# An encoder step on one core: the first chunk opened by row blocks, and six of eight output blocks turned by VectorE

## Chip, core and metric

One core of one Trainium2 chip. The metric is the device time of one launch in microseconds (us), median of three runs. TensorE is called PE, VectorE DVE, ScalarE ACT, GpSimd POOL, SyncE SP.

## What is computed

One step of a two-layer streaming encoder on 256 prompt rows and 32 sample rows, model width 1024, all in float32:

```python
def _trunk(x, p, hgrn_state, sb_k, sb_v):
    for l in range(DEPTH):                                  # 2 layers
        x = x + 0.5 * _swiglu(_rms(x, ffn1_norm[l]), ffn1_w_gate[l], ffn1_w_up[l], ffn1_w_down[l])
        h = _rms(x, mix_norm[l])
        y = _mixer_ab(h, ...) if l % 2 == 0 else _mixer_c(h, ...)
        x = x + y
        x = x + 0.5 * _swiglu(_rms(x, ffn2_norm[l]), ffn2_w_gate[l], ffn2_w_up[l], ffn2_w_down[l])
    return x, ...

def _swiglu(x, w_gate, w_up, w_down):                       # 1024 -> 2816 -> 1024
    return (jax.nn.silu(x @ w_gate) * (x @ w_up)) @ w_down
```

Outputs are `x` of the prompt (256 x 1024) and of the sample (32 x 1024), and caches of the mixers, which the change does not touch.

## The kernel before

`x` lives transposed in SBUF: `xT` has 8 blocks `k` of 128 model columns, each 128 partitions x 288 columns (`NT`: 32 sample rows, then 256 prompt rows). Weights are read once, in a fixed stream of chunks of up to 8 blocks of 128 x 256 (1 MB each). `fetch` loads a chunk into one of three `wraw` buffers from SP's queue; `pieces` splits it, two blocks at a time, into a rounded part `wh` (ACT, line 206) and a rest `wl` (DVE, line 207), which go to four `wspl` buffers of half a chunk each. Every block product takes three matmuls per half of the output columns (lines 246 to 248: `wl` with `xh`, `wh` with `xl`, `wh` with `xh`; here called products), so a chunk of 8 blocks is 48 products of 288 columns. `xh` and `xl` are the same split of `x` times the norm's gain (`gained`: ACT line 291, DVE line 292). The norm's factor `rb` is applied when a result leaves PSUM (`evac`).

The order on each engine is the order of the code, with a few things let in between: `tick`, called after each block, advances the split of the next chunk and, at a rate, the steps of a "lane" (`nlane`) that holds the norm (`rnorm`) or the output of a block (`result`). The loads and stores of SP's and ACT's queues use eight semaphores in turn, and an issue waits until the one eight before it has landed.

The opening: `setup` loads the identity, `x_prompt` in halves of 512 columns (rows 0 to 127 from SP's queue, 128 to 255 from ACT's), `x_sample` from POOL's queue and the first weight chunk in halves (`fetch_half`). `first_block` then turns each block `k` by PE transposes (`turn`, line 1143: 128, 128 and 32 rows into one PSUM tile), splits it, and copies it to `xT` (`keep`). `WARM` is the number of filler matmuls on PE, (8, 6): eight at the start, six after four turns (line 1155). The row sums of squares are made by DVE (`first_squares`). Chunk 0 then runs with all its 48 products, and `rb` is made by a matmul (line 328) in the middle of chunk 1.

The closing: the last step of the last layer's second SwiGLU is four column groups `j` of three chunks (8, 8 and 6 blocks), called c0 to c11 here. `last` runs the two halves of the final chunk of a group one after the other, adds each to `xT` (`resid`, line 359), and queues `result(k)`: three PE transposes back to rows (line 1258), an ACT and a DVE copy out of PSUM, one store of the prompt's part on SP's queue (line 1262, pieces of 512 bytes) and one of the sample's on ACT's.

Of the kernel before, what the change touches and what calls it, by code (L numbers as in the profile page):

```python
# [14 lines left out]
P = 128  # L15
D = 1024
# [77 lines left out]
class Net:  # L94
# [89 lines left out]
    def fetch_half(self, j):  # L184

        if j == 0:
            self.raw[0] = self.t(self.wraw, [P, 8, 256], "wraw")
        x = slice(4 * j, 4 * j + 4)
        ap, = self.stream[0]
        self.nc.sync.dma_start(out=self.raw[0][:, x], in_=ap[4 * j * P:4 * j * P + 4 * P].rearrange("(k p) c -> p k c", p=P))  # L190
# [63 lines left out]
    def in_chunk(self):  # L254
        acc = self.pair_ps()
        ch = self.next_chunk()
        self.mm((acc[:, 0], acc[:, 1]), ch, (self.xh, self.xl), self.KORD, True, True)
        self.nlane.drain()
        return acc

    def evac(self, pool, tag, bufs=None):
        acc = self.in_chunk()
        x = self.t(pool, [P, 2, NT], tag, bufs=bufs)
        self.nc.vector.tensor_tensor(out=x, in0=acc[:, :, :NT], in1=self.rb, op=ALU.mult)  # L264
        return x
# [132 lines left out]
    def ffn(self, gnext):  # L398
        nc = self.nc
        with self.tc.tile_pool(name=f"ffn{self.uid}", bufs=2, reuse_waits="tile") as pool:  # L400
            self.hidden(pool, KF)
            for n in range(DFF // 256):
                if n == 3 and not self.lv:
                    self.constants()
                g = self.evac(pool, "g")
                nc.scalar.activation(out=g, in_=g, func=AF.Silu)  # L406
                u = self.evac(pool, "u")
                nc.vector.tensor_tensor(out=u, in0=u, in1=g, op=ALU.mult)  # L408
                self.put(2 * n, u)
# [668 lines left out]
    def setup(self, st):  # L1078
        nc, I, c = self.nc, self.I, self.const
        self.st = st  # L1080
        xs = [self.t(st, [P, 1472 if i == 0 else D], f"xs{i}") for i in range(3)]
        warm = self.t(st, [P, 8], "warm")
        nc.vector.memset(warm, 0.0)
        nc.scalar.activation(out=warm, in_=warm, func=AF.Copy, scale=1.0)
        xp, xq = I["x_prompt"], I["x_sample"]
# [4 lines left out]
        nc.gpsimd.dma_start(out=xs[2][0:TS], in_=xq[0])  # L1090
        nc.sync.dma_start(out=cf, in_=I["cf"][:, :P])
        nc.scalar.dma_start(out=first, in_=I["ffn1_norm"][0].rearrange("(n p) -> n p", p=P))
# [13 lines left out]
        spare = self.pair_ps()  # L1106
        for i in range(self.WARM[0]):
            nc.tensor.matmul(spare[:, 0, :P], lhsT=self.ones, rhs=self.ones, start=True, stop=True)
        self.onr = c.tile([P, P], F32R, name="onr")
# [10 lines left out]
        pr = self.ps("first")  # L1120
        nc.tensor.transpose(pr[:, :8], first, self.ident[:8, :8])
# [5 lines left out]
        with self.tc.manual_schedule(engines={mybir.EngineType.Activation, mybir.EngineType.DVE}):  # L1127
            self.first_block(st, xs, g0, spare)
        self.nlane.rate = 0.5

    WARM = (8, 6)

    def first_block(self, st, xs, g0, spare):

        nc = self.nc
        split = self.ahead = self.pieces(0)
        px = {}

        def turn(k):
            px[k] = self.ps("x")  # L1140
            for w, n in enumerate(ROWS):
                s = WIN[w][0]
                nc.tensor.transpose(px[k][:, s:s + n], xs[w][:n, k * P:k * P + P], self.ident[:n, :n])  # L1143
# [6 lines left out]
        stats = self.first_squares(st, xs)  # L1150
        next(stats)
        for k in range(4):
            turn(k)
# [3 lines left out]
        keep(0, v)  # L1157
        next(split)
        keep(1, a)
        turn(4)  # L1160
        keep(2, v)
        turn(5)
        next(split)
        keep(3, a)
        turn(6)
        next(split)
        turn(7)
        next(stats, None)
        norm = self.rnorm(None)
        next(norm)  # L1170
        self.nlane.todo.append(norm)
        keep(4, a)
        keep(5, a)
        keep(6, a)
        keep(7, a)

    def first_squares(self, st, xs):

        nc = self.nc
        part = self.t(st, [P, 3, 2, 6], "part")  # L1180
        mv = self.t(st, [P, 3, 2], "mv")
        nc.vector.memset(mv, 0.0)
        for i in range(2):
            for w, n in enumerate(ROWS):
                nc.vector.bn_stats(part[:n, w, i], xs[w][:n, i * 512:i * 512 + 512])
            if i == 0:
                yield
# [5 lines left out]
        nc.vector.tensor_scalar(out=c, in0=c, scalar1=EPS, scalar2=None, op0=ALU.add)  # L1193

    def constants(self):
# [5 lines left out]
        rows = self.t(self.st, [P, D], "xs1")[:, :P]  # L1201
# [108 lines left out]
```

## Time and profile before

| | |
|---|---|
| median of 3 runs | 1337.16 us (1335.19 to 1337.35) |
| profiled execution | 1338.63 us, its span 1336.9 us |
| busy share of the span | PE 100%, DVE 66%, ACT 50%, POOL 3% |
| mean granted PE clock | 0.996 of full speed |
| DMA queues | SP's moves 210.57 MB, its packets took 50.3% of 16 engines' span |

The span is from the first to the last instruction; 1.7 us of the profiled execution lie outside it. Busy shares are averages: PE is busy to the end, but in the first 18 us part of this is at half clock and part is not products.

### The profile page before, as it was taken

The page shows a single profiled execution, that of the slowest core. Times are in us where ns is not written, and L with a number is a line of the kernel's source. Part 1 is how long each engine was busy: PE and PEld are TensorE (multiplying, and loading weights), DVE is VectorE, ACT ScalarE, POOL GpSimd, SP SyncE. Part 2 cuts the span into 40 slices and gives each one's busy share as a digit, 9 for nine tenths or more (in the row PEclk, how much of TensorE's full clock was granted, in tenths as well). Part 3 has the DMA queues.
Part 4 walks back from the last instruction along what each step waited for, and adds up shares of the span by engine and source line. Part 5 has one row for each costly group of instructions (what it writes and reads, how often), then busy time and mean ns, then how long its engine had stood idle before and what let it go on. Part 6 is the DMA issues. An engine that isn't in the chain of part 4 may idle for free.

```text
span 1336.9 us, 24562 instructions
## 1 busy us (share of the span) xinstructions
PE 1330.8 (100%) x10012; PEld 1322.5 (99%) x10012; DVE 879.8 (66%) x1686; ACT 672.8 (50%) x1379; POOL 41.5 (3%) x64
## 2 busy tenths in 40 slices
PE   9999999999999999999999999999999999999998
PEld 8999999999999999999999999999999999999998
DVE  7666555879797856666655666565568966666543
ACT  5544445474747466544444644444565446444432
POOL 0000000011101010000000000020000000000000
PEclk8999999999999999999999999999999999999999
DMA  8555556454535345555555555575544545555551
GB/s 264 176 167 163 158 167 191 139 164 135 160 107 164 103 144 175 173 165 158 159 165 180 160 160 166 180 193 174 164 152 133 160 158 158 179 167 159 160 181 43
DMA packets 215603, 214.70 MB, mean 161 GB/s; under 512 B 4865, under 2 KB 214258, under 8 KB 215490
## 3 DMA queue, kind: packets, MB, share of 16 engines
q1 hardware_dynamic: 214130, 210.57, 50.3%
q0 software_dynamic: 672, 1.90, 0.6%
q8 instruction: 78, 1.28, 0.4%
q10 hardware_dynamic: 688, 0.66, 0.2%
q14 instruction: 35, 0.29, 0.1%
HBM read 208.27 MB, written 4.85 MB: 159 GB/s over the span
## 4 chain that ended last, share of the span: by engine, by line
PE 99%; DMA 0%; issue 0%; DVE 0%; ACT 0%; ACTq 0%; POOLq 0%
PE acc L248 31%; PE acc L247 31%; PE acc L246 31%; PE sc L578 1%; PE sp L1035 1%; PE S L651 0%; DMA xs<-in_x_sample_dram 0%; PE x L1143 0%; PE zs L788 0%; PE sc L606 0%; PE ob L855 0%; PE vt L941 0%; PE kt L141 0%; PE z L800 0%; PE ob L850 0%; PE acc L1155 0%
## 5 line engine op out<-in xcount | busy, mean ns | idle before, releaser
L206 ACT CAST wh<-wraw 128x512 fp32r<-128x512 f32 x768 | 442.1, 619 | 476.3 <-PE acc L248 358.0
L207 DVE TENSOR_TENSOR wl<-wraw,wh 128x512 fp32r<-128x512 f32 x768 | 507.6, 687 | 264.3 <-ACT wh L206 263.5
L246 PE MATMUL acc<-xh,wl 128*128 128x288 f32 x2112 | 634.6, 300 | 0.0
L247 PE MATMUL acc<-xl,wh 128*128 128x288 f32 x2112 | 624.1, 295 | 0.0
L248 PE MATMUL acc<-xh,wh 128*128 128x288 f32 x2112 | 623.9, 295 | 0.0
L247 PEld LDWEIGHTS acc<-xl,wh 128*128 128x128 f32 x2112 | 397.6, 188 | 0.6
L246 PEld LDWEIGHTS acc<-xh,wl 128*128 128x128 f32 x2112 | 397.5, 188 | 0.6
L248 PEld LDWEIGHTS acc<-xh,wh 128*128 128x128 f32 x2112 | 397.1, 188 | 0.0
L246 PE MATMUL acc<-hh,wl 128*128 128x288 f32 x960 | 285.4, 298 | 0.0
L248 PE MATMUL acc<-hh,wh 128*128 128x288 f32 x960 | 283.3, 295 | 0.0
L247 PE MATMUL acc<-hl,wh 128*128 128x288 f32 x960 | 283.0, 295 | 0.0
L246 PEld LDWEIGHTS acc<-hh,wl 128*128 128x128 f32 x960 | 180.2, 188 | 0.8 <-ACT hh L832 0.2
L247 PEld LDWEIGHTS acc<-hl,wh 128*128 128x128 f32 x960 | 180.5, 188 | 0.2
L248 PEld LDWEIGHTS acc<-hh,wh 128*128 128x128 f32 x960 | 180.3, 188 | 0.0
L264 DVE TENSOR_TENSOR u<-acc,rb 128x576 f32<-128x576 f32 x52 | 39.3, 757 | 48.9 <-PE acc L248 48.9
L264 DVE TENSOR_TENSOR g<-acc,rb 128x576 f32<-128x576 f32 x48 | 36.3, 757 | 47.3 <-PE acc L248 47.3
L284 ACT CAST hh<-u 128x576 fp32r<-128x576 f32 x52 | 35.1, 676 | 56.0 <-DVE u L408 41.2
L285 DVE TENSOR_TENSOR hl<-u,hh 128x576 fp32r<-128x576 f32 x52 | 39.4, 758 | 7.6 <-ACT hh L284 1.7
L291 ACT ACTIVATE xh<-xT,cols 128x288 fp32r<-128x288 f32 x40 | 21.2, 531 | 26.5 <-DVE xT L359 15.4
L408 DVE TENSOR_TENSOR u<-u,g 128x576 f32<-128x576 f32 x44 | 33.1, 751 | 0.0
L406 ACT ACTIVATE g<-g 128x576 f32<-128x576 f32 x44 | 30.0, 682 | 0.1
L292 DVE SCALAR_TENSOR_TENSOR xl<-xT,cols,xh 128x288 fp32r<-128x288 f32 x40 | 20.6, 515 | 8.5 <-ACT xh L291 8.5
(299 smaller groups left out, 766.8 us busy)
## 6 DMA issues: line engine op xcount, KB each, us to landing
wraw<-in_ffn_w_up_dram SPq DMA_DIRECT2D x44, 1024.0 KB, 5.6
wraw<-in_ffn_w_gate_dram SPq DMA_DIRECT2D x43, 1024.0 KB, 5.3
wraw<-in_ffn_w_down_dram SPq DMA_DIRECT2D x32, 1024.0 KB, 5.4
wraw<-in_ab_w_in_dram SPq DMA_DIRECT2D x28, 1024.0 KB, 5.2
wraw<-in_c_w_in_dram SPq DMA_DIRECT2D x16, 1024.0 KB, 5.4
wraw<-in_ffn_w_down_dram SPq DMA_DIRECT2D x16, 768.0 KB, 4.5
wraw<-in_c_w_out_dram SPq DMA_DIRECT2D x8, 1024.0 KB, 5.0
wraw<-in_ab_w_out_dram SPq DMA_DIRECT2D x8, 768.0 KB
```

Source lines behind the costliest of these rows:

```text
L206: self.nc.scalar.copy(out=h[:, x], in_=w[:, a:b])
L207: self.nc.vector.tensor_tensor(out=l[:, x], in0=w[:, a:b], in1=h[:, x].bitcast(F32), op=ALU.subtract)
L246: mm(o, lhsT=l[:, k, c], rhs=hi[:, r], start=st, stop=False)
L247: mm(o, lhsT=h[:, k, c], rhs=lo[:, r], start=False, stop=False)
L248: mm(o, lhsT=h[:, k, c], rhs=hi[:, r], start=False, stop=en)
L264: self.nc.vector.tensor_tensor(out=x, in0=acc[:, :, :NT], in1=self.rb, op=ALU.mult)
L284: nc.scalar.copy(out=hh, in_=h)
L285: nc.vector.tensor_tensor(out=self.hl[:, k:k + 2], in0=h, in1=hh.bitcast(F32), op=ALU.subtract)
L291: nc.scalar.activation(out=self.xh[:, k], in_=x, func=AF.Copy, scale=g)
L292: nc.vector.scalar_tensor_tensor(out=self.xl[:, k], in0=x, scalar=g, in1=self.xh[:, k].bitcast(F32), op0=ALU.mult, op1=ALU.subtract)
L406: nc.scalar.activation(out=g, in_=g, func=AF.Silu)
L408: nc.vector.tensor_tensor(out=u, in0=u, in1=g, op=ALU.mult)
```

## The change

The title of the change: opening a row block at a time with the sample turned whole; x's first six blocks go back to rows by VectorE's 32x32 transposes, and stores place the squares.

Opening. `x_prompt` comes in four quarters of 256 columns with both row groups in one load, alternating on SP's queue with four quarters of the first weight chunk (`fetch_part`); the sample comes by ACT's queue into a 128-row tile whose other rows POOL clears, and is turned as a 128-row block. `opening` writes out chunk 0: two turns, then the products of one or two blocks, then the next turns, with the `wl` products last of a block instead of first. Fillers are nine and one. The sums of squares move behind this and are shared between DVE (`bn_stats` of one half) and ACT (`Square` with an accumulator, of the other); `rb` follows at the end of chunk 1 (lane rate 0.2 for 0.5), and chunk 2 takes two PSUM tiles of the `misc` pool. Chunks 1 to 3 are fetched after the opening's loads.

Closing. For `k` below 6 `result` is one DVE transpose of 128 x 288, in squares of 32 x 32, and eight stores on SP's queue that place the squares: four of 32 x 8 x 32 elements (prompt), four of 32 x 32 (sample), in pieces of 32 elements (128 bytes). Blocks 6 and 7 go as before.

```diff
-    def fetch_half(self, j):
+    def fetch_part(self, j):
+        n = self.PIECE
...
+        self.nc.sync.dma_start(out=self.raw[0][:, n * j:n * j + n],
+                               in_=ap[n * j * P:n * (j + 1) * P].rearrange("(k p) c -> p k c", p=P))
...
+    def opening(self):
+        acc = self.pair_ps()
+        self.pos = 1
+        self.due = self.rate = 0.0
...
+        def products(k):
+            h, l = self.spl[0][k // 4]
+            for w, x in ((h, self.xh), (h, self.xl), (l, self.xh)):
+                for b in range(2):
+                    mm(acc[:, b, :NT], lhsT=w[:, k % 4, b * P:b * P + P], rhs=x[:, k],
+                       start=(k == 0 and w is h and x is self.xh), stop=(k == KD - 1 and w is l))
...
-        nc.gpsimd.dma_start(out=xs[2][0:TS], in_=xq[0])
+        nc.scalar.dma_start(out=xq[0:TS], in_=I["x_sample"][0])
...
-        for j in range(2):
-            cs = slice(j * 512, j * 512 + 512)
-            nc.sync.dma_start(out=xs[0][:, cs], in_=xp[0, 0:P, cs])
-            nc.scalar.dma_start(out=xs[1][:, cs], in_=xp[0, P:TP, cs])
-            self.fetch_half(j)
+        for j in range(4):
+            cs = slice(j * 256, j * 256 + 256)
+            nc.sync.dma_start(out=xs[:, :, cs], in_=xp[:, :, cs])
+            self.fetch_part(j)
...
-    WARM = (8, 6)
+    WARM = (9, 1)
...
+        turn(0)
+        next(split)
+        turn(1)
         for i in range(self.WARM[1]):
-            nc.tensor.matmul(spare[:, 1, :P], lhsT=xs[0][:, :P], rhs=xs[1][:, :P], start=True, stop=True)
+            nc.tensor.matmul(spare[:, 0, :P], lhsT=self.ones, rhs=self.ones, start=True, stop=True)
+        products(0)
         next(split)
+        turn(2)
+        turn(3)
+        products(1)
+        keep(0, a)
...
+            nc.vector.bn_stats(part[:n, w], xs[w][:n, 0:512])
+            nc.scalar.activation(out=junk[:n], in_=xs[w][:n, 512:D], func=AF.Square, scale=D ** -0.5,
+                                 accum_out=sa[:n, w:w + 1])
...
+        if k < KD - 2:
+            y = self.t(self.nrm, [P, NT], "sq", bufs=2)
+            nc.vector.transpose(y, self.xT[:, k])
+            for o, a, e in ((O[0][0], TS, NT), (O[1][0], 0, TS)):
+                to = o[:, cs].rearrange("(n t) (a c) -> a t n c", t=TS, a=4)
+                for q in range(4):
+                    nc.sync.dma_start(out=to[q], in_=y[TS * q:TS * q + TS, a:e].rearrange("t (n c) -> t n c", c=TS))
+            yield
+            return
```

PE's first instructions before the change (`acc_97` is filled by fillers, `x_131` to `x_149` are turned blocks, `acc_223` is chunk 0's result):

```order
L1108 MATMUL acc_97<-ones 128x128 x8
L1121 MATMUL first_117<-ident,first_84 128x8
L1143 MATMUL x_131<-ident,xs_1_76 128x128
...
L1143 MATMUL x_149<-ident,xs_2_77 128x128
L1143 MATMUL x_149<-ident,xs_3_78 128x32
L1155 MATMUL acc_97<-xs_2_77,xs_1_76 128x128 x6
L1143 MATMUL x_169<-ident,xs_1_76 128x128
L1143 MATMUL x_169<-ident,xs_2_77 128x128
L1143 MATMUL x_169<-ident,xs_3_78 128x32
L246 MATMUL acc_223<-xh,wl_162 128x288
L247 MATMUL acc_223<-xl,wh_161 128x288
```

and after it (`acc_132` is chunk 0's result, `xs_2_77` the sample):

```order
L1144 MATMUL acc_100<-ones 128x128 x7
L1146 MATMUL first_101<-ident,first_82 128x8
L1144 MATMUL acc_100<-ones 128x128 x2
L1180 MATMUL x_135<-ident,xs_2_77 128x128
L1180 MATMUL x_135<-ident,xs_1_76 128x128 x2
L1180 MATMUL x_145<-ident,xs_2_77 128x128
L1180 MATMUL x_145<-ident,xs_1_76 128x128 x2
L1191 MATMUL acc_100<-ones 128x128
L267 MATMUL acc_132<-xh,wh_141 128x288 x2
L267 MATMUL acc_132<-xl,wh_141 128x288 x2
L267 MATMUL acc_132<-xh,wl_142 128x288 x2
L1180 MATMUL x_160<-ident,xs_2_77 128x128
```

The first product stood behind five turns and fourteen fillers, and stands behind two turns and ten fillers; the sample's part of a turn is 128 columns wide where it was 32.

SP's queue in the closing before the change (`sq_14698` and `sq_14758` are blocks 2 and 3; `wraw_14706`, `wraw_14777`, `wraw_14837` and `wraw_14900` are chunks c8 to c11):

```order
L180 DMA wraw_14706<-in_ffn_w_down_dram 128x6x256
L180 DMA wraw_14777<-in_ffn_w_down_dram 128x8x256
L1262 DMA out_dram<-sq_14698 128x2x128
L180 DMA wraw_14837<-in_ffn_w_down_dram 128x8x256
L1262 DMA out_dram<-sq_14758 128x2x128
L180 DMA wraw_14900<-in_ffn_w_down_dram 128x6x256
```

and after it (`sq_14700` and `sq_14761` are blocks 2 and 3, `wraw_14713`, `wraw_14785`, `wraw_14845` and `wraw_14909` c8 to c11):

```order
L180 DMA wraw_14713<-in_ffn_w_down_dram 128x6x256
L1311 DMA out_dram<-sq_14700 32x8x32 x4
L1311 DMA out_dram<-sq_14700 32x32 x4
L1311 DMA out_dram<-sq_14761 32x8x32 x4
L1311 DMA out_dram<-sq_14761 32x32 x4
L180 DMA wraw_14785<-in_ffn_w_down_dram 128x8x256
L180 DMA wraw_14845<-in_ffn_w_down_dram 128x8x256
L180 DMA wraw_14909<-in_ffn_w_down_dram 128x6x256
```

The fetch of c9 stood ahead of the stores of blocks 2 and 3, and now stands behind all sixteen of them.

## Rows read from the trace of the kernel before

**Rows 1.** The page: busy time by engine, and the chain that ended last by engine.

```profile
PE 1330.8 (100%) x10012; PEld 1322.5 (99%) x10012; DVE 879.8 (66%) x1686; ACT 672.8 (50%) x1379; POOL 41.5 (3%) x64
...
PE 99%; DMA 0%; issue 0%; DVE 0%; ACT 0%; ACTq 0%; POOLq 0%
```

**Rows 2.** Busy time by stretch: the stretch in us and its length, busy us (and instructions) of PE, PE's weight loads, DVE, ACT and POOL, then the granted PE clock, the DMA engines' share and GB/s.

```profile
4.06:7.47 3.41, 2.64 (x15) 1.58 (x13) 2.06 (x5) 0.56 (x2) 0.00 (x0) 1.00 1.06 295
7.47:13.91 6.44, 6.44 (x27) 5.25 (x26) 4.47 (x9) 3.21 (x7) 0.00 (x0) 0.50 1.09 354
13.91:17.71 3.80, 3.80 (x15) 3.06 (x15) 1.99 (x4) 2.46 (x6) 0.00 (x0) 0.50 0.93 316
17.71:25.73 8.02, 8.02 (x61) 7.98 (x61) 7.22 (x20) 5.70 (x13) 1.27 (x1) 1.00 0.71 238
1275.00:1332.00 57.00, 57.00 (x435) 56.88 (x433) 22.97 (x43) 18.32 (x35) 0.00 (x0) 1.00 0.38 118
```

**Rows 3.** The chain that ended last, in order of time, in the first 27 us: start, us, what (the time a step holds the chain, for a matmul the time to the next).

```profile
1.34 5.24 DMA xs<-in_x_sample_dram
...
6.63 1.83 PE x L1143 x7
8.46 2.86 PE acc L1155 x12
11.31 0.67 PE x L1143 x3
11.98 0.54 PE acc L246
...
16.13 0.24 PE acc L246
16.37 1.49 PE x L1143 x6
17.86 0.33 PE acc L247
18.19 0.14 PE acc L248
```

**Rows 4.** PE in order of time: the first fillers, the first product of chunk 1, and the matmul of `rb` in its middle (start, busy us, with the last one's way through the array).

```profile
1.16 3.41 PE L1108 MATMUL acc<-ones 128*128 128x128 f32 x16 [1.16 <-DVE mv L1182]
...
22.54 0.29 PE L246 MATMUL acc<-xh,wl 128*128 128x288 f32 x1
...
25.73 0.65 PE L328 MATMUL rb<-dg,ones 128*128 128x288 f32 x2
```

**Rows 5.** DVE in order of time: its first reads of x's halves (in brackets the idle time before and what ended it), and the last step ahead of `rb`.

```profile
4.63 0.69 DVE L1185 BATCH_NORM_STATS2 part<-xs 128x6 f32<-128x512 f32 x1 [3.48 <-DMA xs<-in_x_prompt_dram]
...
6.11 1.27 DVE L1185 BATCH_NORM_STATS2 part<-xs 128x6 f32<-128x512 f32 x2 [0.72 <-DMA xs<-in_x_prompt_dram]
...
24.64 0.63 DVE L325 TENSOR_SCALAR dg<-ident,pw 128x128 f32<-128x128 f32 x3 [0.80 <-POOL pw L133]
```

**Rows 6.** Groups of instructions on ACT and DVE in the first 40 us, shapes apart, and of the accumulator's read-out in the whole run: busy us, mean ns of one.

```profile
L206 ACT CAST wh<-wraw 128x512 fp32r<-128x512 f32 x22 | 12.8, 628 | 6.7 <-PE acc L248 5.3 <-issue 1.4
L291 ACT ACTIVATE xh<-x,g 128x288 fp32r<-128x288 f32 x8 | 3.9, 502 | 8.5 <-PE x L1143 8.4
L1147 ACT COPY xT<-x 128x288 f32<-128x288 f32 x6 | 2.2, 414 | 0.0
...
L207 DVE TENSOR_TENSOR wl<-wraw,wh 128x512 fp32r<-128x512 f32 x21 | 14.0, 682 | 2.0 <-ACT wh L206 1.9
L292 DVE SCALAR_TENSOR_TENSOR xl<-x,g,xh 128x288 fp32r<-128x288 f32 x8 | 4.0, 517 | 3.7 <-ACT xh L291 3.5
...
L724 ACT ACTIVATION_READ_ACCUMULATOR on<-kt 128x1 f32 x20 | 3.9, 196 | 0.0
```

**Rows 7.** The chain that ended last around the turning back of one block in the closing: start, us, what.

```profile
1300.49 0.13 PE acc L248
1300.62 0.33 PE y L1258 x3
```

**Rows 8.** SP's queue in the closing: start of the fetches of c8 and c9, and us from the first's start to the second's end.

```profile
1285.82 7.34 SPq L180 DMA_DIRECT2D wraw<-in_ffn_w_down_dram  x2
```

**Rows 9.** Issues of stores: ns of an issue (min/median/max), first and last start; time to landing of all of them; and from the page the landing of the closing's fetches (median us) and SP's queue (packets, MB, share of 16 engines).

```profile
L755 SPq DMA_DIRECT2D out_dram<-bvt x8: 419/448/1167, 281.4 to 471.1; - x8
...
L1006 SPq DMA_DIRECT2D out_dram<-vo x4: 592/600/714, 1033.0 to 1035.1; - x4
...
DMA to landing us min/median/max: 1.5/1.9/3.5
...
wraw<-in_ffn_w_down_dram SPq DMA_DIRECT2D x32, 1024.0 KB, 5.4
...
q1 hardware_dynamic: 214130, 210.57, 50.3%
```

**Rows 10.** DVE and ACT in order of time in the closing: the additions of blocks 2 and 5 to x, and the first split of c9.

```profile
1293.16 0.46 DVE L359 SCALAR_TENSOR_TENSOR xT<-acc,xT 128x288 f32<-128x288 f32 x1 [0.39 <-PE acc L248]
...
1305.82 1.14 ACT L206 CAST wh<-wraw 128x512 fp32r<-128x512 f32 x2 [2.56 <-PE acc L248]
...
1314.25 0.45 DVE L359 SCALAR_TENSOR_TENSOR xT<-acc,xT 128x288 f32<-128x288 f32 x1
```

More of the change, by code (lines that the diff above doesn't have):

```diff
@@ L252, with evac @@
     KORD = [(k, k) for k in range(KD)]
-    def in_chunk(self):
-        acc = self.pair_ps()
+    def opening(self):
+        acc = self.pair_ps()
+        self.pos = 1
+        self.due = self.rate = 0.0
+        mm = self.nc.tensor.matmul
+        def products(k):
[4 more added lines that the diff above has]
+                       start=(k == 0 and w is h and x is self.xh), stop=(k == KD - 1 and w is l))
+        with self.tc.manual_schedule(engines={mybir.EngineType.Activation, mybir.EngineType.DVE, mybir.EngineType.PE}):
+            self.first(products)
+        self.spl.pop(0)
+        self.raw.pop(0)
+        return acc
+    def in_chunk(self):
+        if self.pos == 0:
+            return self.opening()
+        if self.pos == 2:
+            acc = tuple(self.ps("acc")[:, :NT] for _ in range(2))
+        else:
+            pair = self.pair_ps()
+            acc = (pair[:, 0], pair[:, 1])
         ch = self.next_chunk()
-        self.mm((acc[:, 0], acc[:, 1]), ch, (self.xh, self.xl), self.KORD, True, True)
+        self.mm(acc, ch, (self.xh, self.xl), self.KORD, True, True)
         self.nlane.drain()
-        return acc
-    def evac(self, pool, tag, bufs=None):
-        acc = self.in_chunk()
+        return acc if self.pos == 3 else pair
+    def evac(self, pool, tag, bufs=None, acc=None):
+        acc = acc or self.in_chunk()
         x = self.t(pool, [P, 2, NT], tag, bufs=bufs)
+        if isinstance(acc, tuple):
+            for b in range(2):
+                self.nc.vector.tensor_tensor(out=x[:, b], in0=acc[b], in1=self.rb[:, b], op=ALU.mult)
+            return x
         self.nc.vector.tensor_tensor(out=x, in0=acc[:, :, :NT], in1=self.rb, op=ALU.mult)
@@ L404, in ffn @@
                     self.constants()
-                g = self.evac(pool, "g")
+                two = [self.in_chunk() for _ in range(2)] if self.pos == 0 else (None, None)
+                g = self.evac(pool, "g", None, two[0])
                 nc.scalar.activation(out=g, in_=g, func=AF.Silu)
-                u = self.evac(pool, "u")
+                u = self.evac(pool, "u", None, two[1])
                 nc.vector.tensor_tensor(out=u, in0=u, in1=g, op=ALU.mult)
@@ L1080, in setup @@
         self.st = st
[L1081 to L1085, printed above, removed]
+        xs, xq = self.t(st, [P, 2, D], "xs0"), self.t(st, [P, D], "xs2")
+        for r in (slice(TS, 64), slice(64, P)):
+            nc.gpsimd.memset(xq[r], 0.0)
         NC = 384 + 384 + PAST + TS + TS
@@ L1126, in setup, with first_block @@
         self.xl = c.tile([P, KD, NT], F32R, name="xl")
-        with self.tc.manual_schedule(engines={mybir.EngineType.Activation, mybir.EngineType.DVE}):
-            self.first_block(st, xs, g0, spare)
-        self.nlane.rate = 0.5
-    WARM = (8, 6)
-    def first_block(self, st, xs, g0, spare):
+        self.first = lambda products: self.first_block(st, (xs[:, 0], xs[:, 1], xq), g0, spare, products)
+        self.nlane.rate = 0.2
+    WARM = (9, 1)
+    def first_block(self, st, xs, g0, spare, products):
         nc = self.nc
-        split = self.ahead = self.pieces(0)
+        split = self.pieces(0)
         px = {}
         def turn(k):
[L1140 to L1143, printed above, removed]
+            px[k] = spare[:, 0] if k == 4 else self.ps("x")
+            for w in (2, 0, 1):
+                s, e = WIN[w]
+                nc.tensor.transpose(px[k][:, s:e], xs[w][:, k * P:k * P + P], self.ident)
             self.gained(k, px[k][:, :NT], g0[:, k:k + 1])
@@ L1192, in first_squares @@
         nc.vector.tensor_tensor(out=c, in0=c, in1=mv[:, :, 1], op=ALU.add)
-        nc.vector.tensor_scalar(out=c, in0=c, scalar1=EPS, scalar2=None, op0=ALU.add)
+        nc.vector.tensor_scalar(out=c, in0=c, scalar1=0.5, scalar2=EPS, op0=ALU.mult, op1=ALU.add)
+        nc.vector.tensor_tensor(out=c, in0=c, in1=sa, op=ALU.add)
+        next(split)
+        norm = self.rnorm(None)
+        next(norm)
+        self.nlane.todo.append(norm)
+        for k in (6, 7):
+            keep(k, a)
     def constants(self):
```

63 lines of the change are left out of this document (30 added, 33 removed).

## Prediction

> **What bounds the kernel now.** I read the page's busy shares and its chain first: PE is busy 1330.8 of 1336.9 us, and the chain that ended last is 99% PE [rows 1]. So work taken from another engine gains nothing, and there are three ways to gain: fewer PE instructions, PE at full clock, or products that start earlier. Then I read the first 26 us by stretch. The granted clock falls to half (1.2 GHz) at 7.47 and comes back to full (2.4 GHz) at 17.71, that is 10.24 us [rows 2]. The chain shows what PE did there: it waited for the sample until 6.59, turned four blocks until 8.46, ran fillers for 2.86 us, and gave the first product only at 11.98 [rows 3]. The first product of chunk 1 starts at 22.54 [rows 4]. The 48 products of chunk 0 need 48 x 0.133 = 6.4 us at full clock (61 PE instructions in 8.02 us there [rows 2]), so some 16 us have gone to the opening. From there PE is full to the last chunk; the only things in the closing that are not products are the turns back, 0.33 us of the chain for each block [rows 7].
>
> **The closing, PE.** Six blocks no longer go through PE: 6 x 0.33 = **2.0 us** less, at full clock and on the chain [rows 7]. Blocks 6 and 7, whose turns and stores end the kernel, are as before.
>
> **The opening.** I walk through the new order with the old durations. A turn of three 128-column transposes is 0.33 us at full clock [rows 7] and 0.67 at half [rows 3]; a product is 0.13 and 0.24 [rows 3]; a split of x 0.50 on ACT and 0.52 on DVE, of two weight blocks 0.63 and 0.68, a copy to `xT` 0.41 [rows 6].
> Fillers: 16 half-instructions took 3.41 us from 1.16 [rows 4]; nine fillers end near 5.0. The first quarter of x is 256 KB behind the identity on SP's queue, as the first half was, which was read at 4.63 [rows 5]; I take that. The sample took 5.24 us by POOL's queue and held the chain until 6.59 [rows 3]; on ACT's queue it stands behind one small load. It lands between 3 (issue near 1.5, and 1.5 us, the shortest landing of a 16 to 128 KB store [rows 9]) and 6.6; I take 5. POOL's clearing of the other rows runs beside this. Then two turns and a filler to 5.9, the split of block 0 by 6.4, the first weight quarter (256 KB, 0.74 us at 354 GB/s [rows 2], behind the first x quarter) split by 6.5 and 7.1, and the six products of block 0 from 6.5 to **7.4**.
> From there on loads are not the limit: a further quarter of x and of weights lands every 1.5 us (512 KB at 354 GB/s [rows 2]), and PE needs 2.3 us for the two blocks in it at full clock. ACT needs 2 x 0.50 + 0.63 + 0.41 = 2.04 and DVE 2 x 0.52 + 0.68 = 1.72 us for them [rows 6], so ACT is close behind PE, but not ahead of it. Left at 7.4 are six turns and 42 products: 6 x 0.33 + 42 x 0.133 = 7.6 us at full clock, which ends chunk 0 at 15.0. Each microsecond at half clock does 0.133 / 0.24 = 0.55 of the products, or half of the turns, and so costs about 0.47.
> How long the half clock lasts I can only bound: by nothing, and by the 10.24 us of before [rows 2]. In before it fell at the end of a stretch in which PE waited for loads (busy 2.64 of 3.41 us, weight loads only 1.58) [rows 2]; the new order still has fillers, two turns, and waits for splits up to 7.4, so I take it that it falls. It came back after 3.80 us in which products and turns stood end to end [rows 2, 3]; ahead of that, turns of 32 columns and fillers stood between [rows 3]. In the new order products and 128-column turns stand end to end from 7.4 on. I take 4 us at half clock: 0.47 x 4 = 1.9, chunk 0 ends at 16.9, and against 22.54 the opening gains **5.6 us**. The ends are 22.54 - 15.0 = 7.5 (never at half) and 22.54 - (15.0 + 4.8) = 2.7 (10.24 us at half).
>
> **Costs behind the opening.** `rb`: its matmul now stands at the end of chunk 1, 6.4 us after chunk 0. The chain ahead of it is ACT's: after the last split of x come six copies of 0.41, seven casts of 0.63, and three squares, for which I take a cast's 0.63 plus a read-out of 0.20 [rows 6]: 2.5 + 4.4 + 2.5 = 9.4 busy us; back to back a second cast adds 1.14 - 0.63 = 0.51 only [rows 6, 10], and with 16 instructions that is some 1.8 us less, so 7.6 to 9.4. Then 0.7 for `wl` and 0.6 for `dg` [rows 5, 6]. The last split of x ends 2.4 us ahead of chunk 0's last product. So `rb` is ready 6.5 to 8.3 us after chunk 0, and PE is there after 6.4: a wait of 0.1 to 1.9 us. PE executes in order, so it delays chunk 2's products, which don't need `rb`. In before `dg` began 1.1 us ahead of the matmul [rows 4, 5]. I take **0.3 us**. Chunk 2 uses other PSUM tiles, so it does not wait for the two results that `rb` holds up.
>
> **The closing, other engines.** DVE's transpose has no row. By the 128 x 288 and 128 x 512 rows it lies between 0.46 and 0.68 us [rows 6, 10]; DVE is busy for 22.97 of the 57 us of the closing [rows 2], and even 2 us each would be covered. The work that covers it is the 17 us of products of a column group. The stores are the point to watch. Per block SP issues eight stores where it issued one. The nearest rows are 0.42 to 0.45 us for a plain store and 0.60 to 0.71 for one with a third dimension [rows 9]: 4 x 0.65 + 4 x 0.45 = 4.4 us, 8.8 for blocks 2 and 3. Behind these stands the fetch of c9. Blocks 2 and 3 can be turned as soon as they are added (1293.16 + 0.5 [rows 10], and some 3 us later), so SP issues from 1294.2 to 1303.0, and c9 is fetched 10 us later than before, when it was the second of two issues that end at 1293.2 [rows 8]. It lands 5.4 us later [rows 9], at 1308.4. ACT's first split of c9 was at 1305.82 [rows 10] and slips by 2.6 us; PE begins c9 at 1313.9 (block 5 is added at 1314.25 [rows 10]) and needs 1.3 us for the first split. 4.2 us of cover are left, so the cost is **nothing**. The engines: a block has 1152 pieces of 128 bytes, 72 on each of 16. A piece of SP's queue took 50.3% x 16 x 1336.9 / 214130 = 50 ns at 983 bytes on average [rows 9]; if a small one is no dearer, 3.6 us, less than SP needs to issue them.
> No store of before has pieces under 512 bytes, so the trace bounds them only from the larger side. The Trainium skill (DMA: Bandwidth & Descriptors, Specifications) speaks against this part: below 512 bytes a DMA reads, modifies and writes. If that doubles a piece (an estimate), two blocks take 14.4 us instead of 8.8, PE would wait 1.4 us for c9, and the gain would be 5.9 instead of 7.3; no row here shows it.
>
> **The sum.** 2.0 + 5.6 - 0.3 = 7.3 us. The profiled execution took 1338.63 us, its span 1336.9, so it would be 1331.3. It lies 1.5 us above the median of the runs, and the same step from the median gives 1337.16 - 7.3 = **1329.9 us**.
>
> **Rivals.**
> (1) The clock never falls: end to end from about 5 us on. For it: the wait for the sample in the middle of the turns is gone, and six products fall into the stretch that had none [rows 2, 3]. Against: PE still waits for splits up to 7.4. 7.5 + 2.0 - 0.4 = 9.1 us: 1328.1.
> (2) The clock stays at half as long as before, 10.24 us, for the new order keeps twelve turns' worth of transposes between products. For it: from 11.31 to 16.37 two turns and eleven products had also followed closely, and the clock was half throughout [rows 2, 3]. Against: it did come back while six transposes ran. 2.7 + 2.0 = 4.7: 1332.5. The Trainium skill (TensorE: Matmul & The Clock Gate, Part 4: PE-mode transpose) says that transposes do not count as PE work for the clock as matmuls do, which would make this one the likelier; the trace bears out neither.
> (3) Slower: the stores. With p us for each store, c9 is split at 1294.2 + 16p + 5.4 + 1.3, and PE waits from p = 0.81 on. The gain of 7.3 is used up at 16p - 13.0 = 7.3, p = 1.27, and at p = 1.6 the time is 1337.16 - 7.3 + 12.6 = 1342.5. Against it: only a single issue of before reached 1.17 us, the medians are 0.38 to 0.60 [rows 9], and landings of 1.5 to 3.5 us [rows 9] are shorter than the eight issues after which a store's semaphore comes round again.
> (4) The opening gains little: loads in smaller pieces land late (sample at 6.6, each quarter some 1.5 us behind my times), so block 0 is done at 9.0, and PE is at half clock to the end of chunk 0: 6 x 0.67 + 42 x 0.24 = 14.1, so it ends at 23.1, 0.6 later than before. With 2.0 from the closing and `rb` 0 to 1.9 us late that is 1335.8 to 1337.7, no difference that can be told.
>
> **How the numbers follow.** Forecast 0.45, (1) 0.20, (2) 0.20, (4) 0.09, (3) 0.06. A measurement of this kernel tells about 0.2% (2.7 us) from no change. The first three are faster by more: 0.85; (4) is the same, 0.09; (3) slower, 0.06. The range takes in (1) and (2), with the spread of the runs of before (1335.19 to 1337.35) on either side: 1326.8 to 1334.0. The likeliest case alone has 1328.6 to 1331.2, from 2 to 6 us at half clock and a wait for `rb` of 0 to 1 us.
>
> **What would show it.** The first product near 6.5 instead of 11.98, and the first product of chunk 1 near 17 instead of 22.54. A stretch at half clock that begins near 7.5 and ends near 11.5. The matmul of `rb` with a wait of under 1 us. In the closing no turn on PE before block 6, and PE without a gap at c9, whose fetch SP issues about 9 us after block 2 was added. The forecast is wrong if the stores' issues take over 0.8 us each, or if the clock is at half for longer than 6 us or not at all.

## The result and the profile after

| | us |
|---|---|
| before, median (6 runs) | 1336.54 (1335.19 to 1338.76) |
| after, median (6 runs) | 1330.19 (1329.92 to 1330.24) |
| ratio | 0.9949, interval 0.9937 to 0.9961 |
| profiled execution of after | 1330.23, its span 1328.5 |

The change makes the kernel 0.5% faster: 1330.19 us where 1329.9 was predicted, and well inside the range. As will be seen, the opening was taken some 2 us too large, and the number came out by luck: the base from which it was subtracted was 1.4 us too high.

The page of after, busy time by engine:

```profile
PE 1322.6 (100%) x9986; PEld 1316.6 (99%) x9986; DVE 878.4 (66%) x1682; ACT 672.7 (51%) x1381; POOL 43.6 (3%) x67
```

PE is busy for 8.2 us less than in [rows 1], and the span is 8.4 us shorter (1336.9 to 1328.5): the gain is PE's. The opening by stretch (columns as in [rows 2]), the last one being 57 us of the closing:

```profile
4.06:7.24 3.18, 2.64 (x16) 2.19 (x14) 0.69 (x3) 1.06 (x3) 0.00 (x0) 1.00 1.05 329
7.24:15.91 8.67, 8.67 (x67) 8.45 (x67) 6.75 (x13) 7.61 (x20) 0.00 (x0) 1.00 1.05 342
15.91:23.38 7.47, 6.97 (x53) 6.66 (x51) 7.17 (x21) 7.08 (x16) 1.24 (x1) 1.00 0.95 294
1268.00:1325.00 57.00, 56.78 (x428) 56.29 (x426) 25.02 (x45) 16.68 (x30) 0.00 (x0) 1.00 0.42 118
```

The granted clock is 1.00 in each stretch; [rows 2] had 10.24 us at 0.50. PE of after in order of time: the last fillers, the first turns, the first products, the first product of chunk 1, and `rb`:

```profile
4.65 1.17 PE L1144 MATMUL acc<-ones 128*128 128x128 f32 x4
5.65 0.82 PE L1180 MATMUL x<-ident,xs 128*128 128x128 f32 x6
...
7.24 0.54 PE L267 MATMUL acc<-xh,wh 128*128 128x288 f32 x2 [0.55 <-ACT wh L207]
...
8.34 0.81 PE L1180 MATMUL x<-ident,xs 128*128 128x128 f32 x6
...
15.91 0.31 PE L247 MATMUL acc<-xh,wl 128*128 128x288 f32 x1
...
23.00 0.75 PE L360 MATMUL rb<-dg,ones 128*128 128x288 f32 x2 [0.50 <-DVE dg L357]
```

The first product starts at 7.24 (11.98 before, [rows 3]), chunk 1 at 15.91 (22.54, [rows 4]), and `rb` at 23.00 (25.73), now with all 48 products of chunk 1 ahead of it instead of 24. The chain of waits in the first 11 us of another execution of after shows what holds the first product (start, us, what):

```profile
...
4.71 0.82 PE acc L1144 x4
5.54 0.34 PE x L1180 x3
...
5.90 0.50 ACT xh L323
6.40 0.52 ACT wh L207
...
6.96 1.26 PE acc L267 x6
```

It is the fillers, the first turn, and then two steps of ACT in a row. No load stands in it. The closing, DVE in order of time: block 0 is added and turned, and block 7 is added:

```profile
1269.00 0.46 DVE L391 SCALAR_TENSOR_TENSOR xT<-acc,xT 128x288 f32<-128x288 f32 x1 [0.45 <-PE acc L249]
1269.49 0.48 DVE L1307 STREAM_TRANSPOSE sq<-xT 128x288 f32<-128x288 f32 x1
...
1324.02 0.46 DVE L391 SCALAR_TENSOR_TENSOR xT<-acc,xT 128x288 f32<-128x288 f32 x1 [1.95 <-PE acc L249]
```

A DVE transpose takes 0.47 to 0.48 us. From the addition of block 0 to that of block 7 it is 55.02 us. In the trace of the kernel before it is 56.98, 1.96 more:

```profile
1274.96 0.46 DVE L359 SCALAR_TENSOR_TENSOR xT<-acc,xT 128x288 f32<-128x288 f32 x1 [0.45 <-PE acc L248]
...
1331.94 0.46 DVE L359 SCALAR_TENSOR_TENSOR xT<-acc,xT 128x288 f32<-128x288 f32 x1 [1.94 <-PE acc L248]
```

SP's queue in the closing, and the issues of the new stores:

```profile
1287.53 7.63 SPq L1311 DMA_DIRECT2D out_dram<-sq  x16
1295.26 3.20 SPq L180 DMA_DIRECT2D wraw<-in_ffn_w_down_dram  x3
```
```profile
L1311 SPq DMA_DIRECT2D out_dram<-sq x48: 314/434/1401, 1270.0 to 1314.8; - x48
...
DMA to landing us min/median/max: 1.4/1.6/3.2
```

Sixteen stores hold the queue for 7.63 us, 0.48 each, and the fetch of c9 follows at 1295.26, 8.7 us after block 2 was added (1286.54). ACT waits for it, and splits it at once:

```profile
1301.63 2.19 ACT L207 CAST wh<-wraw 128x512 fp32r<-128x512 f32 x4 [5.70 <-DMA wraw<-in_ffn_w_down_dram]
```

PE's waits in the whole run, behind the first one (for the fillers' data, at the start):

```profile
PE acc L267 <- ACT wh L207: 0.5, 1, 0.5
PE rb L360 <- DVE dg L357: 0.5, 1, 0.5
PE y L1317 <- DVE xT L391: 0.2, 1, 0.2
```

None is in the closing, but for block 7's turn.

### The profile page after: what moved, and what is told of

Its sections match the earlier page's. It is cut to its first block, busy times and chain, and to the rows that moved or that the text cites. A ratio compares the mean times of both kernels' runs of the same rounds, so it can differ in the third digit from the quotient of the medians.

```text
span 1328.5 us, 24573 instructions
## 1 busy us (share of the span) xinstructions
PE 1322.6 (100%) x9986; PEld 1316.6 (99%) x9986; DVE 878.4 (66%) x1682; ACT 672.7 (51%) x1381; POOL 43.6 (3%) x67
## 2 busy tenths in 40 slices
DMA packets 221907, 214.70 MB, mean 162 GB/s; under 512 B 12385, under 2 KB 221074, under 8 KB 221794
## 4 chain that ended last, share of the span: by engine, by line
PE 98%; DMA 1%; DVE 0%; SPq 0%; issue 0%; ACT 0%; DVEq 0%
PE acc L249 30%; PE acc L248 30%; PE acc L247 30%; PE sc L612 1%; DMA wraw<-in_ffn_w_up_dram 1%; PE sp L1069 1%; PE S L685 0%; PE zs L822 0%; PE sc L640 0%; PE ob L889 0%; PE vt L975 0%; PE kt L141 0%; PE z L834 0%; PE ob L884 0%; DVE wl L208 0%; SPq L190 0%
```

## Experiments

Runs of one set are on one chip, with their own runs of the kernel before beside them. The median of that is 1335.84, 1335.62, 1335.80 and 1335.66 in the four sets, close enough that times are compared across sets to some tenths. After itself ran again at 1329.88.

**The opening alone.** `result` turns every block on PE as before; the rest is the change.

```diff
-        if k < KD - 2:
+        if k < 0:
```

> The changed opening with the closing of before (PE turns all eight blocks back). Theory (two independent parts, 2.0 us of PE time in the closing): 2.0 us over the changed kernel, 1332.2 us. The tail behind the last product was 0.5 us shorter in the changed kernel's trace; if that belongs to the closing too, 1332.7. Rival (the closing gains nothing, all comes from the opening): 1330.2.

Measured 1332.43 (ratio 0.9971, 0.9959 to 0.9982). Against the change as a whole (1330.19), the six blocks are worth 2.2 us.

**The closing alone.** The kernel before, with the new branch of `result` put in front.

> The opening of before with the changed closing. Theory: 2.0 to 2.5 us under the kernel before, 1334.0 to 1334.5 for its median of 1336.5, with that kernel's spread of some 3 us. Rival (the stores cost PE time that the opening's gain hides in the changed kernel): 1336.5 or more.

Measured 1333.84 (0.9987, 0.9978 to 0.9997), 2.0 us under the kernel before. Both agree with 6 x 0.33 us of [rows 7], and the two traces with the opening changed have the same 2.0 at one place: block 7 is added at 1326.02 without the new closing, at 1324.02 with it, and block 0 within 0.03 us of the same time in both.

**The kernel before, once more.** No edit.

> The kernel before once more, for the clock of each run. Theory (its spread of 1335.2 to 1338.8 us is the length of the half-clock stretch in the opening, at some 0.47 us for each us of it): the runs fall on one line of time against mean clock; a run of 1338.6 has 0.996 (10.2 us at half), one of 1335.4 has 0.998 to 0.999 (about 3.4 us). Rival (the spread comes from loads): the clocks are alike and the times differ.

Median 1335.75 (1335.42 to 1337.28), profiled execution 1335.55. This is the run that told most. Its PE in order of time:

```profile
10.42 0.40 PE L246 MATMUL acc<-xh,wl 128*128 128x288 f32 x1
...
22.56 0.72 PE L328 MATMUL rb<-dg,ones 128*128 128x288 f32 x2 [0.60 <-DVE dg L325]
```

and its stretches:

```profile
5.00:10.50 5.50, 4.91 (x29) 3.60 (x29) 4.91 (x11) 3.22 (x7) 0.00 (x0) 1.00 1.07 338
10.50:20.00 9.50, 9.50 (x68) 8.87 (x69) 8.04 (x20) 8.23 (x19) 0.00 (x0) 1.00 1.03 328
```

The clock does not fall. `rb` comes at 22.56, 3.17 us ahead of [rows 4], and this execution is 3.08 us shorter than the one I had predicted from. So the old order of work does not bring the 10.24 us at half clock by itself. They make a mean clock of 0.996, and of the 96 executions with the old opening whose clock is on record only two have that: the one that I had predicted from, and one of the closing alone (1336.48, 3.1 us over its profiled one). None of the 50 with the new opening has it (the doubled stores below are left out), which is too few to say that the new opening prevents it.

What was expected of the runs did not come out. They do not fall on one line of time against clock: 1337.28 has 1.000, 1335.82 has 0.998. Of the 75 runs of the kernel before that stand beside the experiments or are these ten, 12 lie between 1337.1 and 1337.6, and ten of the 12 have 1.000. That does not clear the clock either, since its column reads 1.00 too while PE starts at half pace (last section). No trace of such a run was kept, so why they are some 1.6 us longer stays open.

**Twice the issues.** Each new store is split in two, so that a block takes 16 issues of half the size.

```diff
-                    nc.sync.dma_start(out=to[q], in_=y[TS * q:TS * q + TS, a:e].rearrange("t (n c) -> t n c", c=TS))
+                    src = y[TS * q:TS * q + TS, a:e].rearrange("t (n c) -> t n c", c=TS)
+                    n = (e - a) // TS
+                    for i in range(2):
+                        if n > 1:
+                            s = slice(i * n // 2, i * n // 2 + n // 2)
+                            nc.sync.dma_start(out=to[q][:, s], in_=src[:, s])
+                        else:
+                            s = slice(16 * i, 16 * i + 16)
+                            nc.sync.dma_start(out=to[q][s], in_=src[s])
```

> The changed kernel with every store of the six blocks cut in two, so 96 issues for 48 with the same bytes and pieces. Theory (SP's issues delay the fetch of c9): the sixteen issues took 7.6 us, so c9 comes 7.7 us later; PE had 3.3 us of cover between the first split of c9 and its first product, so PE waits 4.4 us there: 1334.6. Rival (the pieces in the DMA engines set the pace, or the fetch has more cover): 1330.2.

Measured 1339.07 (ratio 1.0022, 1.0013 to 1.0031): slower than before. PE's waits, and SP's queue in its closing:

```profile
PE acc L247 <- DVE wl L208: 6.9, 2, 4.6
```

```profile
1297.88 0.40 SPq L180 DMA_DIRECT2D wraw<-in_ffn_w_down_dram  x1
...
1306.83 1.02 SPq L180 DMA_DIRECT2D wraw<-in_ffn_w_down_dram  x2
```

The fetch of c9 now stands at 1306.83, 11.6 us later than in after where 7.7 were expected: sixteen issues take 8.2 to 10.2 us of the queue. PE waits 4.6 us for it. c8's, at 1297.88, is late too (2.35 us), which I had not expected: in this kernel it stands behind the stores of block 2, in after it stood ahead of them. So the second wait is near the 4.4 expected only because the first had already put PE back. Behind the longer wait PE has half its pace for 3 us, as its own rows and the clock of the stretch show:

```profile
1313.70 0.61 PE L247 MATMUL acc<-hh,wl 128*128 128x288 f32 x1 [4.59 <-DVE wl L208]
...
1316.75 0.38 PE L247 MATMUL acc<-hh,wl 128*128 128x288 f32 x1
```
```profile
1300.00:1320.00 20.00, 13.05 (x85) 12.59 (x85) 8.77 (x15) 6.02 (x11) 0.00 (x0) 0.91 0.52 150
```

Twelve products take 3.05 us there, some 1.4 more than at 0.13 each. Block 7 is added 9.0 us later than in after: 6.9 are waits, 1.4 the clock, and 0.6 are not accounted for. So the mechanism of the slower rival is real, and the change stays on the good side of it by the length of SP's queue.

**The sample turned narrow.** The changed kernel with the sample's part 32 rows wide, and last of its turn instead of first.

```diff
-            for w in (2, 0, 1):
-                s, e = WIN[w]
-                nc.tensor.transpose(px[k][:, s:e], xs[w][:, k * P:k * P + P], self.ident)
+            for w, n in enumerate(ROWS):
+                s = WIN[w][0]
+                nc.tensor.transpose(px[k][:, s:s + n], xs[w][:n, k * P:k * P + P], self.ident[:n, :n])
```

> The changed kernel as it is, as the measure for the three others of this set: 1329.9 to 1330.3 us as before. Theory A (the new opening keeps PE at full clock from about 5.6 us on, in each execution): no run above 1330.8. Rival (the quiet runs so far were luck): a spread of 2 to 3 us, as the kernel before had.

> The changed kernel with the sample turned as 32 rows, as before. In the trace of the kernel before run again two turns between products took 1.03 us (12.83 to 13.86), with 0.17 us of idle weight loading ahead of each 32-row part; in the changed kernel two whole turns took 0.57 (8.34 to 8.91). Theory A: each narrow turn costs 0.2 us more on PE; six stand behind the first product, so chunk 1 starts 1.2 us later (near 17.1 for 15.91). rb becomes ready at 22.9 as now, since its chain begins with the last quarter of the first weight chunk, so its 0.5 us wait goes, and the time is 0.7 us longer: 1330.9. Rival: the width is worth nothing, and chunk 1 starts at 15.9 and the time is 1330.2. Rival: the narrow turns let the clock fall in the opening: a stretch at half clock in the trace, 1331.5 to 1333.5 and runs spread over 2 us.

Measured 1329.88 for after, with no run above 1330.19, as its Theory A has it; but the kernel before has no run above 1336.37 beside it either. The narrow sample has 1331.35 (1330.69 to 1332.63, and one run at 1335.29). Its profiled execution is 1330.69, 0.98 over that of after in this set (1329.71). Its PE in order of time:

```profile
8.00 1.10 PE L1180 MATMUL x<-ident,xs 128*128 128x128 f32 x6
9.03 0.53 PE L267 MATMUL acc<-xh,wh 128*128 128x288 f32 x2
...
16.96 0.29 PE L247 MATMUL acc<-xh,wl 128*128 128x288 f32 x1
```

Two narrow turns take 1.03 us where two whole ones take 0.57 (8.34 to 8.91 above), chunk 1 starts at 16.96, and `rb` has no PE wait any more. Theory A holds in each of these. The median is another half microsecond above it, and the scatter is wider than after's (1329.62 to 1330.19); all seven have a granted clock of 1.000, and no trace shows the run at 1335.29, so what the narrow turns do beyond their own length stays open.

**The sample by POOL's queue.** The changed kernel; the load is issued ahead of POOL's clearing.

```diff
+        nc.gpsimd.dma_start(out=xq[0:TS], in_=I["x_sample"][0])
...
-        nc.scalar.dma_start(out=xq[0:TS], in_=I["x_sample"][0])
```

> The changed kernel with the sample fetched by POOL's queue, as before. It held PE until 6.59 in the kernel before; now the first turn starts at 5.65. Theory A: the first turn starts 0.6 to 0.9 us later, the first product near 8.0, chunk 1 near 16.7; the wait for rb (0.5 us) shrinks by the same and hides most of it: 1330.3 to 1330.6. Rival: all of it shows, 1330.9 to 1331.1. Rival: the sample's landing does not hold the first turn, no difference.

Measured 1330.02: no difference. The first turn starts at 5.66, right behind the fillers. ACT's queue, which I had counted as one of the gains, is worth nothing here, where the fillers run as long as that.

**`dg` one step earlier.**

```diff
-        self.nlane.rate = 0.2
+        self.nlane.rate = 0.25
```

> The changed kernel with lane rate 0.25 for 0.2: dg is written one step earlier, ahead of one weight split instead of behind it, and rb's matmul stands where it stood, at the end of chunk 1. Theory A (rb waits for dg because dg stands behind that split): dg is done near 22.0, PE waits for nothing there, rb's matmul starts near 22.4 instead of 23.0, and the time is 0.5 us shorter: 1329.7. Rival (the power ahead of dg is what comes last): the wait stays, 1330.2.

Measured 1329.70 (1329.08 to 1329.88). PE's waits no longer list `rb`, so the mechanism is as expected; of its 0.5 us, 0.2 are seen, and the runs overlap those of after.

**Before, with the sample whole and by ACT's queue.** The kernel before with the change's sample: loaded by ACT's queue, cleared by POOL, and turned whole and first.

```diff
-        nc.gpsimd.dma_start(out=xs[2][0:TS], in_=xq[0])
+        for r in (slice(TS, 64), slice(64, P)):
+            nc.gpsimd.memset(xs[2][r], 0.0)
...
+        nc.scalar.dma_start(out=xs[2][0:TS], in_=xq[0])
...
-            for w, n in enumerate(ROWS):
-                s = WIN[w][0]
-                nc.tensor.transpose(px[k][:, s:s + n], xs[w][:n, k * P:k * P + P], self.ident[:n, :n])
+            for w in (2, 0, 1):
+                s, e = WIN[w]
+                nc.tensor.transpose(px[k][:, s:e], xs[w][:, k * P:k * P + P], self.ident)
```

> The kernel before with two parts of the change alone: the sample by ACT's queue, cleared by POOL to 128 rows, and turned whole, sample first. Everything else (halves of x and weights, fillers 8 and 6, squares, places of the products) is as before. In the kernel before run again the sample held the first turn until 6.31 and the first product came at 10.42; a narrow turn took 0.52 us for 0.29. Theory A (the old opening ends where rb's chain ends, and that begins with the second weight half, split from 13.59 and then rb at 22.56, whatever PE does ahead of it): the first product comes 1 to 2 us earlier, PE waits as much longer for rb (2 to 3 us for 0.6), and the time is that of before, 1335.3 to 1335.8. Rival (PE's own path sets the end of the opening): the time falls by what PE gains, to 1333.3 to 1334.3.

Measured 1335.74: no difference (0.9997, 0.9987 to 1.0007). The time is Theory A's, its first step is not:

```profile
6.03 2.79 PE L1145 MATMUL x<-ident,xs 128*128 128x128 f32 x12 [0.88 <-DMA xs<-in_x_sample_dram]
...
11.36 0.38 PE L246 MATMUL acc<-xh,wl 128*128 128x288 f32 x1
...
23.05 0.72 PE L328 MATMUL rb<-dg,ones 128*128 128x288 f32 x2 [0.94 <-DVE dg L325]
```

The sample came little sooner by this queue: PE has it at 6.03, and had it at 6.31 in the kernel before run again. There it held only its own parts, and the turns had begun at 5.07; here it is turned first and holds them all. The first product came 0.94 us later, not earlier. `rb` came only 0.49 later. The chain of waits to `rb` shows why, here and in the kernel before run again (this kernel first):

```profile
3.23 10.86 DMA wraw<-in_ffn_w_up_dram
...
14.11 0.63 ACT wh L206
```
```profile
3.61 9.96 DMA wraw<-in_ffn_w_up_dram
13.59 0.63 ACT wh L206
```

The load at its head is not a part of the first weight chunk, as three of my expectations say, but chunk 1 (`w_up`): its first split stands on ACT and DVE ahead of the last splits of x and of the last row sums, and what stands behind it waits for the load too. It starts at 14.11 instead of 13.59, 0.52 later, and `rb` follows it at the same distance. So in the old opening a first product 0.9 us later cost nothing of its own. That an earlier one would gain nothing is likely by the same chain, but this run did not make one.

**`rb` in the middle of chunk 1.** The changed kernel with `rb`'s matmul where it stood before.

```diff
-        self.mm(acc, ch, (self.xh, self.xl), self.KORD, True, True)
+        if self.pos == 2:
+            with self.tc.manual_schedule(engines={mybir.EngineType.PE}):
+                self.mm(acc, ch, (self.xh, self.xl), self.KORD, True, True)
+        else:
+            self.mm(acc, ch, (self.xh, self.xl), self.KORD, True, True)
...
-        self.nlane.rate = 0.2
+        self.nlane.rate = 0.5
```

> The changed kernel with rb's matmul in the middle of chunk 1, where it stood before (lane rate 0.5, and PE in the order of the code for that chunk); all else is the changed kernel. Theory A (rb's chain ends near 22 us in either opening, since it hangs on the last piece of the first weight chunk, and the new opening gains because 24 more products stand ahead of rb's matmul): PE reaches it near 19.1 and waits 2.9 us, chunk 2 starts some 2.3 us later than in the changed kernel, the time is 1332.2. Rival (the opening gains because its first product is 3 us earlier, wherever rb stands): rb's chain moves up with its earlier place in the code, the wait stays near 0.5, and the time 1329.9 to 1330.3.

Measured 1333.73 (1332.47 to 1333.99). The profiled execution is 1332.47:

```profile
22.03 0.75 PE L364 MATMUL rb<-dg,ones 128*128 128x288 f32 x2 [2.40 <-DVE dg L361]
```

PE waits 2.40 us, and `rb` is there at 22.03, hardly ahead of the 22.56 of the kernel before, though the first product came 2.8 us sooner (7.61 for 10.42). Theory A holds: of the opening's gain over 2 us are lost by the place of this one matmul. Moreover the four runs with a granted clock of 1.000 have 1332.47 to 1332.53, the six with 0.998 or 0.999 have 1333.69 to 1333.99, 1.3 us more. The profiled one is of the four, and its clock stays at 1.00 behind the wait; that in the others it falls there is likely, but no trace shows it.

**Fillers: two less, and almost none.** The first is the changed kernel with rate 0.25 and `WARM = (7, 1)`, the second the changed kernel with `WARM = (2, 0)` and the turn of `first` behind the second filler.

> The changed kernel with lane rate 0.25 (as in the run with dg earlier, 1329.7 us) and seven fillers at the start for nine. In the chain of the changed kernel the fillers run to 5.54, at half clock, and the first turn, the split of x and the split of the weights follow them without a gap, so they hold the first product. Theory A: two fillers less let the first turn start 0.4 us earlier and the first product come near 6.9 instead of 7.3; rb's dg is not earlier than 22.2, so 0.2 us at most are gained: 1329.5. Rival (the fillers are what brings the clock up): the turns run at half clock and the first product comes no earlier, 1329.7 to 1330.2.

> The changed kernel (lane rate 0.2) with two fillers at the start and none between the turns and the first products, for nine and one. PE then has next to nothing to do until x lands near 4.3. Theory A (PE comes to full clock by the work it has done since its start, fillers or not): the first turns start near 4.5 and run at half clock (0.67 us each), and half clock lasts until 7 to 10 us; each microsecond of it from then costs 0.47, so the opening is 0.5 to 1.5 us longer and the time 1330.2 to 1331.5. Rival B (the clock is up by 5.6 us whatever PE does): the first product near 6.6, the time 1329.7 to 1330.2. Rival C (without fillers it stays at half or falls in the opening, as in the profiled execution of before, for some 10 us): 1333 to 1334.

With two less the time is 1329.48 (ratio 0.9950, 0.9935 to 0.9965), the lowest median of all. The first turn now waits for the sample, and the first product for ACT's split, as in after:

```profile
5.00 1.09 PE L1180 MATMUL x<-ident,xs 128*128 128x128 f32 x6 [0.34 <-DMA xs<-in_x_sample_dram]
...
6.86 0.54 PE L267 MATMUL acc<-xh,wh 128*128 128x288 f32 x2 [0.55 <-ACT wh L207]
```

It is 0.4 us better than after in a median of four runs each, on another chip, and 0.2 better than with the higher rate alone (1329.70): a step in the right direction, not one that this measurement can tell. With almost none it is 1331.39, 1.5 more than after:

```profile
7.03 0.85 PE L267 MATMUL acc<-xh,wh 128*128 128x288 f32 x2 [0.46 <-ACT wh L207]
...
8.64 1.49 PE L1180 MATMUL x<-ident,xs 128*128 128x128 f32 x6
...
11.85 0.49 PE L1180 MATMUL x<-ident,xs 128*128 128x128 f32 x3
12.10 0.51 PE L267 MATMUL acc<-xh,wh 128*128 128x288 f32 x2
```

A turn takes twice as long until 11.4 (two turns in 1.14 us at 8.64, for 0.57 in after), and from 11.85 on PE has its full pace. The first product comes no sooner (7.03). So the fillers do their work: PE has full pace at about 5.5 with them and at 11.5 without. Theory A, with its later end. The time varies with the execution: in that of the narrow sample, with the same nine fillers, the last two took 0.62 us from 4.57, where they took 1.00 from 4.65 in after.

## Why the prediction was right, and where it was not

**The closing** is right in each step: 2.0 to 2.2 us, no turn on PE ahead of block 6, the transposes on DVE at 0.47 within the bounds taken. A store takes 0.48 to 0.53 us of SP's queue for the 0.55 assumed. c9 has landed at 1301.63, its first split takes 1.3 us, and PE wants it at about 1306.4, just ahead of block 5's addition at 1306.65: some 3.5 us of cover are left for the 4.2 predicted. The Trainium skill (DMA: Bandwidth & Descriptors, Specifications) says that below 512 bytes a DMA reads, modifies and writes, and the changed kernel has 12385 packets below 512 bytes, for 4865 before; no cost of it shows here: the stores land in 1.4 to 3.2 us, as those of before did in 1.5 to 3.5 [rows 9], and in the closing no fetch or store on SP's queue waits for one of them. The issues hold it, as the doubled stores show: with half the size they take 0.51 to 0.64 us each, no less, and PE waits.

**`rb`**: 0.50 us of wait for 0.3 predicted, within 0.1 to 1.9. It is small because 48 products stand ahead of it. The chain ahead of it was not the one worked out: that began with the last split of x and had no load in it, the one in the trace begins with the load of chunk 1 (below).

**The opening's order** came near: first product at 7.24 for 6.5, held not by loads, but by the fillers, which end at 5.65 for the 5.0 taken, and by ACT, which splits x and the weights one after the other (5.90 to 6.92 in the chain above) where I had both done at 6.5. The first six products end at 8.34, and the six turns and 42 products behind them take 7.57 us, where 7.6 were worked out at full clock, and 0.47 more for each microsecond at half.

**The step that failed is the clock.** I took it that the clock falls at 7.5 and stays at half for 4 us. It did not fall: rival (1) in this point, with chunk 1 at 15.91 between its 15.0 and the forecast's 16.9. Beside that, I measured the gain from a stretch at half clock in the profile of before that most executions of before do not have. Against that execution the change did gain more than predicted, 8.4 us by the spans, since the clock did not fall. Against an undisturbed one the opening gains not 5.6 but 2.8 (block 0 is added at 1271.85 there and at 1269.00 in after), or 3.4 by the medians (1335.84 and 1332.43), and with the closing's 2.2 that is 5.6 to the predicted 7.3.

```profile
1271.85 0.46 DVE L359 SCALAR_TENSOR_TENSOR xT<-acc,xT 128x288 f32<-128x288 f32 x1 [0.45 <-PE acc L248]
```

The profiled execution of before lay 1.5 us above its median, which the prediction said, and it subtracted the gain read from that execution from the median without asking which part of the gain was the excess. The median of those three runs, 1337.16, was in turn 1.3 to 1.5 us above those of the later sets (1335.62 to 1335.84): two of the three, 1337.16 and 1337.35, lie among the longer runs, of which there are 12 in 75. So 1337.16 - 7.3 and 1335.8 - 5.6 both end near 1330: an error in the base and one in the gain cancelled, and that was luck.

**What the opening's gain rests on** was not in the prediction either. In the old opening and in the new one `rb`'s chain starts where chunk 1 has landed and its first split, which stands ahead of the row sums on ACT and DVE, can run: 13.59 in the one, 14.36 in the other, and `rb` comes 8.6 to 9.0 us behind:

```profile
6.39 7.95 DMA wraw<-in_ffn_w_up_dram
...
14.36 0.05 ACT wh L207
```

(the chain of waits of after). ACT had been idle for 0.63 and 0.28 us when the load landed, so an earlier landing could bring `rb` forward by little more; the rest is the work queued behind it. So the new opening does not make `rb` earlier, 23.00 against 22.56. The old one let PE wait there with 24 products of chunk 1 behind it; the new one has these 24, 3.2 us, done by then, and 3.2 less the 0.44 is the 2.8 us gained. The earlier first product alone is not enough: with the early place for `rb` the undisturbed time is 1332.47, which loses over 2 us of it. The later place alone could save the old opening little more than the 0.60 us that PE waited there; that was not run. Whether row sums ahead of chunk 1's split would bring `rb` forward was not tried.

## What to carry to other kernels

Before subtracting a gain read from one profiled execution, ask whether the stretch that it removes is in other executions too: here two executions of one kernel differed by 3.1 us in the opening alone. In a start-up, look for the value that arrives last whatever the order is (here the norm's factor, queued behind a split that waits for a load), and move independent work ahead of its consumer; starting earlier alone is not enough. When a store is broken into many issues, count the issues on the queue and the fetch behind them, not the bytes.

## What the runs showed of the hardware

- A transpose of 32 rows is not cheaper than one of 128 on PE: a turn with one took 0.52 us in the run with the narrow sample, against 0.29 with three of 128 in after. In the kernel before run again the weight loading is idle for 0.17 us ahead of the 32-row part:

```profile
11.36 0.13 PEld L1143 LDWEIGHTS x<-ident,xs 32*128 32x128 f32 x1 [0.17 <-issue]
```

- The granted clock in the rows reads 1.00 from the start of the span, while the fillers and first turns run at half pace, until 5.5 us with nine fillers (after) and until some 11.5 us with two. In a start-up the pace of equal instructions tells more than the clock's column.
- A wait of PE in a full stretch can cost more than its length: with the doubled stores twelve products ran at half pace behind one of 4.6 us (clock 0.91 over 20 us). Behind the 2.35 us ahead of it, and behind the 2.40 us of the profiled run with `rb` early, products kept their 0.13 us.
